# Four sigmoid gates of a hybrid layer: 512x1024x1024 products feature-major in eight blocks, or token-major with three of them by Strassen's seven products

## The chip, the core and the metric

The kernel runs on one core of a Trainium2 chip. The time is that of one execution on the device, in microseconds, and the number to compare is the median over several runs. On the core, TensorE (PE in the profile, with PEld for its weight loads) does the matrix products, VectorE (DVE) and ScalarE (ACT) do elementwise work, and transfers from DRAM are issued mostly on SyncE's queue (SP).

## The reference, cut to what matters

The kernel computes two blocks on 512 tokens of width 1024. The change touches the end of the second one:

```python
proj = h @ w_in                                   # h: 512 x 1024, normalised tokens
(..., gates) = jnp.split(proj, points, axis=-1)   # gates: 512 x 4096
ys = jnp.stack([y_a, y_b, y_c, y_d], axis=0)      # four branches, each 512 x 512
branch_d = jnp.einsum('nbsw,nwd->bsnd', ys, w_branch)
g = jax.nn.sigmoid(gates.reshape(bsz, s, N_BRANCH, d))
merged = jnp.sum(g * branch_d, axis=2)            # 512 x 1024
return x + merged @ w_out                         # then a last rms_norm
```

For each of four branches there is thus a gate, sigmoid of a product 512x1024x1024, and a branch product 512x512x1024 by which it is multiplied. The sum over branches goes through `w_out`; the block's own input `x`, the residual, is added.

## The kernel before, in words

**Arithmetic.** Every fp32 product is made of three passes in a reduced fp32 type: each operand is a high part and a low part, and high·high, high·low and low·high are summed in one PSUM bank (`mm3`; its matmuls all have line L264). The tokens are kept transposed, features on the partitions, as `HH` and `HL` (8 blocks of 128x512). A unit of work is a *piece* of weights, 128x1024 numbers: 8 blocks of 128x128 as stationary operand, with the tokens moving (feature-major result), or 2 blocks of 128x512 as moving operand, with the tokens stationary (token-major result). Either way a piece costs 24 matmuls of 512 columns when all 512 tokens take part.

**Weights.** SyncE's queue loads them, 1 MB at a time (two pieces), into three buffers `raw` (L207). For each piece ACT writes the high part, `whi` (L240), and DVE subtracts to get the low part, `wlo` (L241). `whi` and `wlo` are rings of WB = 3 pieces; the program order asks for the split of a piece LA = 2 pieces ahead of its matmuls (`wget`, `pump`), and a raw buffer is loaded anew when its last piece has been split (`used`).

**Order.** One list of items is run in order by `run`; at each item the side generators (`gmlp`, `topk`, `fox`, `dsa`, which make the branches' inputs) are advanced by a step. After the projections named in `MID` come the branches in the order `BRANCHES = (0, 2, 3, 1)`. For each, `gates(n)` gives four times: two gate pieces (`gt_item`, 24 matmuls each, one bank, evacuated by ACT's sigmoid) and one branch piece (`wb_item`, 24 matmuls, two banks, evacuated by DVE: multiply, L1612, and add to the running sum `mg`, L1617). So there are 32 gate pieces and 16 branch pieces. All results are feature-major: after the last branch each row block of `mg` is split in high and low part (`split_slot`: ACT, then DVE on L290) and is then the stationary operand of the last product, `wout_final("w2")`, 192 matmuls. Then `after2` adds the residual `XT`, which has lain in SBUF slots since the block's start, normalises and stores.

**Other names.** `presplit` splits the four inputs `yb` of a branch (L290). SBUF working tiles are slots of 128x512 fp32, `slot_...`; `CST` holds an identity for transposes on PE, which stand on L1108 and L1315 in this kernel.

Of the kernel before, what the change touches and what calls it, by code (L numbers as in the profile page):

```python
# [18 lines left out]
NT = S // 128  # L19
# [26 lines left out]

MID = ("ki qi0 qi1 au0 az0 au1 az1 au2 az2 au3 az3 dv dq0 dk0 dq1 dk1 bc bq0 dz0 dq2 dk2 bq1 cc0 cx0 cb0 cz0 "
# [3 lines left out]
def plan():  # L51


    def gates(n):
        r = []
        for p in range(4):
            r += [f"gt{n}_{2 * p}", f"gt{n}_{2 * p + 1}", f"wb{n}_{p}"]
        return r
# [14 lines left out]
    for n in BRANCHES:  # L73
        g += gates(n)
    g += [f"w2{h}_{j}" for j in range(4) for h in range(2)]
    g = [(n, 1024) for n in g]
    tail = [g[i:i + 2] for i in range(0, len(g), 2)]
# [6 lines left out]
def kernel(  # L84
# [98 lines left out]
    flat = []  # L183
    for r, items in enumerate(raws):
        o = 0
        for name, w in items:
            flat.append((name, r, o, w))
            o += w
    split_ids = {}
# [9 lines left out]
    ws = {"dma": 0, "split": 0, "next": 0}  # L199

    def dma_raw():
        r = ws["dma"]
        if r >= len(raws):
            return
        o = 0
        for w in [k for _, k in raws[r]] if r < 4 else [sum(k for _, k in raws[r])]:
            nc.sync.dma_start(raw_t[r % RAWB][:, o:o + w], wts[r, :, o:o + w])  # L207
            o += w
        ws["dma"] += 1

    def used(r):
        left[r] -= 1
        if left[r] == 0:
            dma_raw()

    def pump(upto):
        while ws["split"] <= min(upto, len(flat) - 1):
            i = ws["split"]
            name, r, o, w = flat[i]
            if i in in_slots:  # L220
                src = raw_t[r % RAWB]
                hs, ls = [get(), get()], [get(), get()]
                for kk in range(2):
                    c = slice(o + kk * 512, o + (kk + 1) * 512)
                    with tc.high_priority():
                        A.activation(hs[kk].r, src[:, c], AF.Copy)
                        V.tensor_sub(ls[kk].r, src[:, c], hs[kk].r)
# [4 lines left out]
            if i not in split_ids:  # L232
# [3 lines left out]
                continue  # L236
            s = split_ids[i] % WB
            src = raw_t[r % RAWB][:, o:o + w]
            with tc.high_priority():
                A.activation(whi[s][:, 0:w], src, AF.Copy)  # L240
                V.tensor_sub(wlo[s][:, 0:w], src, whi[s][:, 0:w])  # L241
# [13 lines left out]
    def adaget(name):  # L255
# [4 lines left out]
        return raw_t[r % RAWB], r  # L260


    def mm(o, l, r, start, stop):
        T.matmul(o, l, r, start=start, stop=stop)  # L264
# [765 lines left out]
    def wout_final(prefix, src, after):  # L1030


        presplit(src, range(8))
        bk = [[bget() for _ in range(2)] for _ in range(NT)]
# [774 lines left out]
```

## Time and profile before

| | |
|---|---|
| runs | 1137.42, 1135.6, 1137.52 us; median 1137.42 |
| the profiled execution: own time, span | 1135.7 us, 1133.9 us |
| PE busy | 1110.3 us, 98% of the span, 5253 matmuls |
| PE weight loads busy | 920.1 us, 81% |
| DVE busy | 726.1 us, 64% |
| ACT busy | 598.5 us, 53% |
| DMA | 118.5 MB, 105 GB/s over the span |

The profile shows one execution. Busy times are sums over instructions, where overlapping ones count once. An instruction's duration runs from its start to the end of its own results; instructions of one engine overlap, so the distance from one start to the next can be shorter than the duration. An engine is idle until the latest of what its next instruction needs has come. The stretch from about 809 to 1083 us of the span holds the gate products, and the last product follows until 1126 us.

### The profile page before, as it was taken

To read this page: it belongs to the slowest core of one execution; us is meant where nothing else is said; L and a number is where in the kernel's file an instruction comes from. 1 tells how busy PE (TensorE), PEld (TensorE's weight loads), DVE (VectorE), ACT (ScalarE), POOL (GpSimd) and SP (SyncE) were. 2 spreads that over 40 slices of the span, in tenths; PEclk is the share of its full clock that TensorE was granted. 3 is DMA by queue.
4 is the path that set the end of the run, shared out by engine and by line. 5 is a ranking of instruction groups with operands and counts; after the bars stand their busy time and mean duration, and the time that the engine had idled before them with its cause. 6 is when DMAs were issued, how large, how long until landed. Compare 5 with 4: busy or idle time off the path is not lost.

```text
span 1133.9 us, 13788 instructions
## 1 busy us (share of the span) xinstructions
PE 1110.3 (98%) x5253; PEld 920.1 (81%) x5253; DVE 726.1 (64%) x1476; ACT 598.5 (53%) x944; POOL 65.1 (6%) x73
## 2 busy tenths in 40 slices
PE   6999999999999999999999999999999999999997
PEld 4788888888878878788887888888888888888886
DVE  7977788763778556789798736555545434443435
ACT  6595497944677365553256434655766333223323
POOL 1330210101320000000000000000000000000000
PEclk9999999999999999999999999999999999999999
DMA  9734223223122452132232222222222322323202
GB/s 327 275 139 156 75 94 130 92 95 110 40 75 78 143 188 74 39 107 107 84 112 94 84 84 82 105 75 75 75 75 75 112 92 94 112 93 112 94 37 75
DMA packets 25422, 118.54 MB, mean 105 GB/s; under 512 B 2950, under 2 KB 3206, under 8 KB 13964
## 3 DMA queue, kind: packets, MB, share of 16 engines
q1 hardware_dynamic: 24780, 116.61, 29.3%
q10 hardware_dynamic: 576, 1.05, 0.2%
q8 instruction: 41, 0.67, 0.2%
q14 instruction: 25, 0.20, 0.1%
HBM read 115.54 MB, written 2.11 MB: 104 GB/s over the span
## 4 chain that ended last, share of the span: by engine, by line
PE 81%; DVE 9%; ACT 4%; issue 3%; POOL 2%; DMA 1%; SPq 0%; POOLq 0%; DVEq 0%; ACTq 0%
PE bank L264 79%; DVE slot L422 2%; ACT slot L105 1%; DVE slot L1267 1%; ACT whi L240 1%; ACT L105 1%; DVE wlo L241 1%; POOL slot L848 1%; DVE best L1266 1%; PE bank L1315 1%; DVE slot L290 1%; POOL slot L847 1%; DMA raw<-in_wts_dram 1%; DMA slot<-in_x_dram 0%; DVE slot L1079 0%
## 5 line engine op out<-in xcount | busy, mean ns | idle before, releaser
L264 PE MATMUL bank<-HH,whi 128*128 128x512 f32 x960 | 371.6, 394 | 1.4 <-ACT HH L105 1.2
L264 PE MATMUL bank<-HH,wlo 128*128 128x512 f32 x960 | 367.6, 390 | 0.0
L264 PE MATMUL bank<-HL,whi 128*128 128x512 f32 x960 | 366.2, 390 | 0.0
L240 ACT ACTIVATE whi<-raw 128x1024 fp32r<-128x1024 f32 (+1 forms) x170 | 178.7, 1052 | 310.6 <-PE bank L264 273.4
L241 DVE TENSOR_TENSOR wlo<-raw,whi 128x1024 fp32r<-128x1024 f32 (+1 forms) x170 | 206.4, 1215 | 194.6 <-ACT whi L240 185.7
L264 PEld LDWEIGHTS bank<-HH,whi 128*128 128x128 f32 x960 | 179.7, 188 | 40.3 <-ACT HH L105 4.4
L264 PEld LDWEIGHTS bank<-HH,wlo 128*128 128x128 f32 x960 | 180.2, 188 | 38.2
L264 PEld LDWEIGHTS bank<-HL,whi 128*128 128x128 f32 x960 | 180.3, 188 | 36.2
L105 ACT ACTIVATE slot<-slot 128x512 fp32r<-128x512 f32 (+4 forms) x179 | 100.5, 589 | 108.8 <-DVE slot L1660 26.0
L105 ACT ACTIVATE slot<-bank 128x512 f32<-128x512 f32 (+7 forms) x275 | 127.6, 491 | 43.5 <-PE bank L264 18.8
L264 PE MATMUL bank<-slot,slot 128*128 128x128 f32 (+5 forms) x755 | 133.5, 320 | 4.5 <-ACT slot L105 4.5
L264 PEld LDWEIGHTS bank<-slot,slot 128*128 128x128 f32 (+2 forms) x755 | 110.2, 186 | 20.1 <-issue 4.2
L105 ACT ACT_TABLE_LOAD x93 | 119.3, 1283 | 3.0 <-PEq L1798 0.7
L264 PE MATMUL bank<-slot,whi 128*128 128x512 f32 x272 | 85.4, 390 | 0.0
L264 PE MATMUL bank<-whi,slot 128*128 128x512 f32 x256 | 81.6, 394 | 0.2 <-ACT slot L105 0.2
L264 PEld LDWEIGHTS bank<-slot,whi 128*128 128x128 f32 x272 | 50.9, 188 | 10.8
L264 PEld LDWEIGHTS bank<-whi,slot 128*128 128x128 f32 x256 | 48.0, 188 | 10.9 <-ACT slot L105 1.1
L264 PE MATMUL bank<-slot,wlo 128*128 128x512 f32 x144 | 56.2, 390 | 0.0
L290 DVE TENSOR_TENSOR slot<-slot,slot 128x512 fp32r<-128x512 f32 x74 | 50.1, 685 | 9.4 <-ACT slot L105 9.2
L264 PE MATMUL bank<-wlo,slot 128*128 128x512 f32 x128 | 49.9, 390 | 0.0
L264 PE MATMUL bank<-whi,HL 128*128 128x512 f32 x120 | 47.1, 392 | 1.3 <-DVE HL L290 1.3
L264 PE MATMUL bank<-whi,HH 128*128 128x512 f32 x120 | 47.3, 394 | 0.6 <-ACT slot L105 0.5
(210 smaller groups left out, 1023.9 us busy)
## 6 DMA issues: line engine op xcount, KB each, us to landing
raw<-in_wts_dram SPq DMA_DIRECT2D x89, 1024.0 KB, 4.8
slot<-in_adw_dram SPq DMA_DIRECT2D x32, 256.0 KB, 6.3
slot<-in_x_dram SPq DMA_DIRECT2D x16, 256.0 KB, 4.5
raw<-in_wts_dram SPq DMA_DIRECT2D x8, 448.0 KB, 6.1
slot<-in_rows_dram SPq DMA_DIRECT2D x10, 256.0 KB, 3.8
slot<-CUM SPq DMA_DIRECT2D x4, 256.0 KB, 3.2
out_dram<-slot SPq DMA_DIRECT2D x4, 256.0 KB, 2.5
out_dram<-slot ACTq DMA_DIRECT2D x4, 256.0 KB, 2.3
```

The source lines that it names most:

```text
L105: return A.activation(o, i, func, **kw)
L240: A.activation(whi[s][:, 0:w], src, AF.Copy)
L241: V.tensor_sub(wlo[s][:, 0:w], src, whi[s][:, 0:w])
L264: T.matmul(o, l, r, start=start, stop=stop)
L290: V.tensor_sub(dst_l, src, dst_h)
L422: V.tensor_tensor_reduce(junk[i % 2].f, ada[k][i].f, cb[i % 2].f, 1.0, 0.0, ALU.mult, ALU.add, mds[k][:, i:i + 1])
L847: G.tensor_copy(d.f[:, 0:sh], src.f[:, 0:sh])
L848: G.tensor_add(d.f[:, sh:512], src.f[:, sh:512], src.f[:, 0:512 - sh])
L1266: V.max(best, sc.f[:, 0:n])
L1267: V.match_replace(sc.f[:, 0:n], best, sc.f[:, 0:n], MARK)
L1315: T.transpose(tb[:, cs], P[u1].f[:, cs], IDENT)
```

## The change

**Token-major gates.** Gate and branch product of all four branches are made with the tokens stationary and 512 output columns (a half) at a time. The first branch, 0, is a plain product (`plain_gate`, `wb_items`): 24 matmuls per piece as before, four banks per half.

**Seven products.** The gates of branches 2, 3 and 1 are cut in quarters, 256 tokens and 512 inputs by 512 inputs and 512 outputs, and made by Strassen's seven products in Winograd's form (`strassen_gate`, products in the order 1, 5, 6, 3, 7, 2, 4). A product has two pieces of 12 matmuls. The weights' combinations are formed in place in the raw buffers by DVE (`prep`) before they are split; the tokens' combinations S1 to S4 are formed once, by a new side generator in the first branch (`sums_work`), S4 in place of a quarter of `HH`, `HL`. Results are summed in PSUM where possible, copied by ACT or added by DVE where a part is used twice.

**Buffers.** As four raw quarters are in use at once, three more raw buffers, of four slots each, are added (`add_buf`); operations on them are 512 columns wide, two to a piece. To free slots, the residual is stored to DRAM (`XD`) after `av` and loaded again before `after2`.

**The sum transposed.** As `mg` is now token-major, `merged_T` transposes it on PE, 32 blocks of 128x128, in three places: 8 after each of the two pieces of product 4 of the last branch and 16 in the middle of the first half of the last product, which takes its pieces in another order.

The diff, cut to its core (`n` counts branches, `V` is DVE, `A` and `act` are ACT, `T` is PE):

```diff
+PRODUCTS = ((1, "11"), (5, "11"), (6, "11"), (3, "22"), (7, "12"), (2, "21"), (4, "11"))
...
+    n = BRANCHES[0]
+    for hf in (1, 0):
+        g += [f"gt{n}_{hf}_{j}" for j in range(4)] + half(n, hf)
+    pairs = [g[i:i + 2] for i in range(0, len(g), 2)]
+    for n in BRANCHES[1:]:
+        pairs += [[f"B{n}_11"], [f"B{n}_12"], [f"B{n}_22"], half(n, 1), [f"B{n}_21"], half(n, 0)]
+    pairs += [["w20_0", "w20_1"], ["w21_0", "w21_1"], ["w20_2", "w21_2"], ["w20_3", "w21_3"]]
+    tail = [[(n, 2048 if n[0] == "B" else 1024) for n in p] for p in pairs]
...
+            if name[0] == "B":
+                quarter[name[1:]] = r
+                n, q = name[1:].split("_")
+                for p, src in PRODUCTS:
+                    if (q == "22" and p not in (2, 4)) or (q == "21" and p in (2, 4)):
...
+        left[r] = {"11": 8, "12": 2, "22": 4, "21": 4}[name[-2:]]
...
+    def add_buf():
+        pool.append(Buf())
+        dma_raw()
...
+    def prep(i):
+        if i >= len(flat) or flat[i][0][0] != "P":
+            return
+        p, n, j = flat[i][0][1], flat[i][0][3], int(flat[i][0][5])
+        args = {"5": ("11", "12"), "6": ("11", "22"), "7": ("12", "22"), "4": ("11", "21")}.get(p)
+        if args is None:
+            return
+        rd, ra = (quarter[f"{n}_{q}"] for q in args)
+        d, a_ = raw_b[rd], raw_b[ra]
+        w = width(1024, d, a_)
+        for o in range(j * 1024, (j + 1) * 1024, w):
+            with tc.high_priority():
+                V.tensor_sub(d.at(o, w), a_.at(o, w), d.at(o, w))
+        if p in "74":
+            used(ra)
...
+            while ws["prep"] <= i + 1:
+                prep(ws["prep"])
+                ws["prep"] += 1
...
+                n = width(w, b)
+                for c in range(0, w, n):
+                    A.activation(whi[s][:, c:c + n], b.at(o + c, n), AF.Copy)
+                    V.tensor_sub(wlo[s][:, c:c + n], b.at(o + c, n), whi[s][:, c:c + n])
...
+        for n, (j, h) in enumerate(first):
+                if between and n == 2:
+                    between()
...
+    XD = dram.tile([512, 1024], F32, name="XD")
+    def x_block(t, h):
+        return XD[t * 128:(t + 1) * 128, h * 512:(h + 1) * 512]
+    for t in range(NT):
+        for h in range(2):
+            nc.sync.dma_start(x_block(t, h), XT[t, h].f)
+            put(XT.pop((t, h)))
...
+    def sums_work():
...
+        for q in range(2):
+            yield from room(6)
+            s1.append(get())
+            d = pair(s1, q)
+            V.tensor_add(d, qv(HH, 1, 0, q), qv(HH, 1, 1, q))
+            V.tensor_add(d, d, qv(HL, 1, 0, q))
+            V.tensor_add(d, d, qv(HL, 1, 1, q))
+            yield
+        for q in range(2):
+            yield from room(6)
+            s2.append(get())
+            d = pair(s2, q)
+            V.tensor_sub(d, pair(s1, q), qv(HH, 0, 0, q))
+            V.tensor_sub(d, d, qv(HL, 0, 0, q))
+            yield
+        yield from room(6)
+        split_sum("S1", s1)
...
+        while "plain" not in D:
+            yield
+        for q in range(2):
+            act(qv(HH, 1, 0, q), pair(s4, q), AF.Copy)
+            V.tensor_sub(qv(HL, 1, 0, q), pair(s4, q), qv(HH, 1, 0, q))
+        put(*s4)
+        sums["S4"] = True
+        while raw_more[0]:
+            yield from room(10)
+            add_buf()
+            raw_more[0] -= 1
+            yield
...
+            def mmf(j=j):
+                if j == 0:
+                    hold["b"] = [bget() for _ in range(NT)]
+                h, l = wget(f"gt{n}_{hf}_{j}")
+                for kk in range(2):
+                    k = 2 * j + kk
+                    c = slice(kk * 512, (kk + 1) * 512)
+                    for t in range(NT):
+                        ts_ = slice(t * 128, (t + 1) * 128)
+                        mm(hold["b"][t][:], HH[:, k, ts_], h[:, c], k == 0, False)
+                        mm(hold["b"][t][:], HH[:, k, ts_], l[:, c], False, False)
+                        mm(hold["b"][t][:], HL[:, k, ts_], h[:, c], False, k == 7)
...
+    def merged_T(hf, ks):
+        bs = [bget() for _ in ks]
+        for b, k in zip(bs, ks):
+            for t in range(NT):
+                T.transpose(b[:, t * 128:(t + 1) * 128], mg[t, hf].f[:, k * 128:(k + 1) * 128], IDENT)
+        for b, k in zip(bs, ks):
+            h, l = get(), get()
+            split(h.r, l.r, b[:])
+            merged[4 * hf + k] = h, l
...
+        def out(i, hf, part, banks_, free):
+            for t in range(2):
+                if part:
+                    s = part[t]
+                    V.tensor_add(s.f, s.f, banks_[t][:])
+                    act(s.f, s.f, AF.Sigmoid)
                 else:
...
+                    s = get()
+                    act(s.f, banks_[t][:], AF.Sigmoid)
+                if free:
+                    bput(banks_[t])
+                sg[2 * i + t, hf] = s
...
+                    h, l = wget(f"P{p}n{n}_{j}")
+                    for kk in range(2):
+                        k = 2 * j + kk
+                        c = slice(kk * 512, (kk + 1) * 512)
+                        for t in range(2):
+                            ah, al = stat(p, k, slice(t * 128, (t + 1) * 128))
+                            go = {} if opens else {"skip_group_check": True}
+                            mm(to[t][:], ah, h[:, c], opens and k == 0, False, **go)
+                            mm(to[t][:], ah, l[:, c], False, False, **go)
+                            mm(to[t][:], al, h[:, c], False, k == 3, **go)
+                def ev():
+                    if p == 1:
+                        copies(p1, X)
+                        presplit_yb(n)
+                    elif p == 5:
+                        copies(p5, Z)
+                    elif p == 6:
+                        copies(u2, X)
+                    elif p == 3:
+                        out(0, 1, u2, Z, True)
+                    elif p == 7:
+                        out(1, 1, p5, X, False)
+                    elif p == 2:
+                        out(0, 0, p1, Y, True)
+                    else:
+                        out(1, 0, None, X, True)
...
+        for p in (1, 5, 6, 3, 7):
+            r += product(p)
+        r += wb_items(n, 1) + product(2)
+        a4 = product(4)
+        if last:
+            a4 = [a4[0], (None, lambda: merged_T(1, (0, 1)), None), a4[1], (None, lambda: merged_T(1, (2, 3)), None)]
+        return r + a4 + wb_items(n, 0)
...
+    run(items, limit=4)
+    sides.append(sums_work())
+    n = BRANCHES[0]
+    items = []
+    for hf in (1, 0):
+        items += plain_gate(n, hf) + wb_items(n, hf)
+    for n in BRANCHES[1:]:
+        items += strassen_gate(n)
...
+    for t in range(NT):
+        for h in range(2):
+            XT[t, h] = get()
+            nc.sync.dma_start(XT[t, h].f, x_block(t, h))
...
-    wout_final("w2", merged, after2)
+    wout_final("w2", merged, after2, (4, 5, 6, 7, 0, 1, 2, 3), ((0, 0), (1, 0), (0, 1), (1, 1)),
+               lambda: merged_T(0, (0, 1, 2, 3)))
```

Three pieces of the program follow, before and after, in the order in which each engine executes. First DVE, before, in the gates of a branch; the names are those of the text above (`bank_` is PSUM):

```order
L241 TENSOR_TENSOR wlo_120<-raw_115,whi_117 128x1024
L241 TENSOR_TENSOR wlo_121<-raw_113,whi_118 128x1024
L1612 TENSOR_TENSOR slot_7092<-slot_7092,bank_63 128x512
L1617 TENSOR_TENSOR slot_6724<-slot_6724,slot_7092 128x512
L290 TENSOR_TENSOR slot_7557<-slot_6208,slot_7556 128x512
L290 TENSOR_TENSOR slot_7561<-slot_6264,slot_7560 128x512
L1612 TENSOR_TENSOR slot_7121<-slot_7121,bank_61 128x512
L1617 TENSOR_TENSOR span_6757<-span_6757,slot_7121 128x512
L241 TENSOR_TENSOR wlo_119<-raw_113,whi_116 128x1024
L241 TENSOR_TENSOR wlo_120<-raw_114,whi_117 128x1024
```

And DVE after, in the last branch, from the split of the first piece of product 6 (`wlo_121<-slot_6876`) to that of the first piece of product 3 (`wlo_120<-raw_113`); L309 is the split, L276 `prep`, here for product 4, L1801 and L1806 are multiply and add for the branch before:

```order
L309 TENSOR_TENSOR wlo_121<-slot_6876,whi_118 128x512
L1801 TENSOR_TENSOR slot_7603<-slot_7603,bank_67 128x512
L276 TENSOR_TENSOR slot_6876<-raw_114,slot_6876 128x512
L309 TENSOR_TENSOR wlo_121<-slot_6877,whi_118 128x512
L309 TENSOR_TENSOR wlo_119<-slot_6878,whi_116 128x512
L276 TENSOR_TENSOR slot_6877<-raw_114,slot_6877 128x512
L276 TENSOR_TENSOR slot_6878<-raw_114,slot_6878 128x512
L309 TENSOR_TENSOR wlo_119<-slot_6879,whi_116 128x512
L1806 TENSOR_TENSOR slot_6772<-slot_6772,slot_7603 128x512
L276 TENSOR_TENSOR slot_6879<-raw_114,slot_6879 128x512
L1801 TENSOR_TENSOR slot_7605<-slot_7605,bank_66 128x512
L309 TENSOR_TENSOR wlo_120<-raw_113,whi_117 128x1024
```

The splits of pieces were one operation of 1024 columns each, alone or around six operations of 512; now those of a quarter that lies in slots are two operations of 512 columns, and `prep`'s subtractions stand between them as well. From the split of product 5's first half piece to that of product 3's first piece there are 23 operations of 512 columns and the one of 1024.

PE before, from the last branch product to the last product:

```order
L264 MATMUL bank_61<-slot_7560,whi_116 128x512
L264 MATMUL bank_61<-slot_7561,whi_116 128x512
L264 MATMUL bank_61<-slot_7560,wlo_119 128x512
L264 MATMUL bank_68<-whi_117,slot_7621 128x512
L264 MATMUL bank_68<-wlo_120,slot_7621 128x512
L264 MATMUL bank_68<-whi_117,slot_7622 128x512
L264 MATMUL bank_64<-whi_117,slot_7621 128x512
L264 MATMUL bank_64<-wlo_120,slot_7621 128x512
L264 MATMUL bank_64<-whi_117,slot_7622 128x512
```

PE after, within product 4 of the last branch (L332 are the products' matmuls, L1817 the transposes of `mg`):

```order
L332 MATMUL bank_65<-whi_116,HH 128x512
L332 MATMUL bank_65<-wlo_119,HH 128x512
L332 MATMUL bank_65<-whi_116,HL 128x512
L1817 MATMUL bank_68<-CST,slot_6475 128x128
L1817 MATMUL bank_68<-CST,slot_6477 128x128
L1817 MATMUL bank_68<-CST,span_6479 128x128
L1817 MATMUL bank_68<-CST,slot_6481 128x128
L1817 MATMUL bank_64<-CST,slot_6475 128x128
L1817 MATMUL bank_64<-CST,slot_6477 128x128
L1817 MATMUL bank_64<-CST,span_6479 128x128
L1817 MATMUL bank_64<-CST,slot_6481 128x128
L332 MATMUL bank_62<-whi_117,HH 128x512
```

The last product followed the last branch product directly; now blocks of eight transposes, which read the sum's slots as DVE left them, stand between products of the last branch, and sixteen more inside the last product.

SP's queue before, at the end (L1024 loads the last normalisation's row, L207 weights, L1670 stores the output):

```order
L1024 DMA slot_7918<-in_rows_dram 128x512
L1024 DMA span_7917<-in_rows_dram 128x512
L207 DMA raw_113<-in_wts_dram 128x2048
L207 DMA raw_114<-in_wts_dram 128x2048
L207 DMA raw_115<-in_wts_dram 128x2048
L207 DMA raw_113<-in_wts_dram 128x2048
L207 DMA raw_114<-in_wts_dram 128x2048
L207 DMA raw_115<-in_wts_dram 128x2048
L207 DMA raw_113<-in_wts_dram 128x1024
```

SP's queue after, before the last weights (`XD` is the residual kept in DRAM):

```order
L1092 DMA slot_8107<-in_rows_dram 128x512
L1092 DMA slot_8106<-in_rows_dram 128x512
L1955 DMA slot_8110<-XD 128x512
L1955 DMA slot_8112<-XD 128x512
L1955 DMA span_8116<-XD 128x512
L245 DMA raw_113<-in_wts_dram 128x2048
L245 DMA slot_6853<-in_wts_dram 128x512
```

The loads of the residual stand between loads of weights, the first three of them ahead of `raw_113`, which holds the first pieces of the last product; each such load waits for its slot to be free.

## Rows read from the trace of the kernel before

**Rows 1.** The page: busy time of engines, and clock by slices.

```profile
PE 1110.3 (98%) x5253; PEld 920.1 (81%) x5253; DVE 726.1 (64%) x1476; ACT 598.5 (53%) x944; POOL 65.1 (6%) x73
...
PEclk9999999999999999999999999999999999999999
```

**Rows 2.** The page: the whole chain by line.

```profile
PE bank L264 79%; DVE slot L422 2%; ACT slot L105 1%; DVE slot L1267 1%; ACT whi L240 1%; ACT L105 1%; DVE wlo L241 1%; POOL slot L848 1%; DVE best L1266 1%; PE bank L1315 1%; DVE slot L290 1%; POOL slot L847 1%; DMA raw<-in_wts_dram 1%; DMA slot<-in_x_dram 0%; DVE slot L1079 0%
```

**Rows 3.** Chain from 880 us on: start, us, what.

```profile
879.90 246.67 PE bank L264 x1087
...
1126.60 0.70 DVE slot L1660
```

**Rows 4.** Stretches: length, then PE, PEld, DVE, ACT, POOL busy, clock, DMA, GB/s.

```profile
440.00:480.00 40.00, 38.49 (x182) 31.07 (x181) 33.57 (x95) 23.43 (x55) 0.00 (x0) 1.00 0.08 27
810.00:876.00 66.00, 66.00 (x320) 55.40 (x319) 31.31 (x65) 42.22 (x64) 0.00 (x0) 1.00 0.23 80
892.00:954.00 62.00, 62.00 (x275) 51.34 (x274) 27.04 (x32) 19.14 (x24) 0.00 (x0) 1.00 0.26 95
```

**Rows 5.** PE's timeline, tokens moving: start, us; 38 rows between.

```profile
903.14 0.39 PE L264 MATMUL bank<-HH,whi 128*128 128x512 f32 x1
...
911.98 0.39 PE L264 MATMUL bank<-HH,whi 128*128 128x512 f32 x1
```

**Rows 6.** PE's timeline, tokens stationary; 8 rows between.

```profile
556.14 0.39 PE L264 MATMUL bank<-wlo,HH 128*128 128x512 f32 x1
...
558.18 0.39 PE L264 MATMUL bank<-wlo,HH 128*128 128x512 f32 x1
```

**Rows 7.** PE's timeline at transposes, and all of that line (busy, mean ns).

```profile
467.72 1.47 PE L1108 MATMUL bank<-CST,slot 128*128 128x128 f32 x12
469.22 0.50 PE L264 MATMUL bank<-whi,HH 128*128 128x512 f32 x1
469.56 0.39 PE L264 MATMUL bank<-wlo,HH 128*128 128x512 f32 x1
...
L1108 PE MATMUL bank<-CST,slot 128*128 128x128 f32 x32 | 4.4, 274 | 0.0
```

**Rows 8.** DVE by line, 892 to 954 us: busy, mean ns, idle before.

```profile
L241 DVE TENSOR_TENSOR wlo<-raw,whi 128x1024 fp32r<-128x1024 f32 x12 | 14.7, 1223 | 30.7 <-ACT whi L240 30.7
L1612 DVE TENSOR_TENSOR slot<-slot,bank 128x512 f32<-128x512 f32 x8 | 5.5, 688 | 6.5 <-PE bank L264 6.5
L1617 DVE TENSOR_TENSOR slot<-slot,slot 128x512 f32<-128x512 f32 x7 | 4.8, 692 | 0.2
```

**Rows 9.** DVE's timeline where it works without a pause.

```profile
345.32 1.28 DVE L530 TENSOR_TENSOR slot<-slot 128x512 f32<-128x512 f32 x2
346.52 1.28 DVE L290 TENSOR_TENSOR slot<-slot,slot 128x512 fp32r<-128x512 f32 x2
...
349.24 1.23 DVE L241 TENSOR_TENSOR wlo<-raw,whi 128x1024 fp32r<-128x1024 f32 x1
350.38 0.69 DVE L647 TENSOR_TENSOR slot<-bank,CST 128x512 f32<-128x512 f32 x1
```

**Rows 10.** ACT by line, 892 to 954 us: busy, mean ns, idle before.

```profile
L240 ACT ACTIVATE whi<-raw 128x1024 fp32r<-128x1024 f32 x12 | 12.7, 1061 | 38.4 <-PE bank L264 34.5 <-issue 3.9
L105 ACT ACTIVATE slot<-bank 128x512 f32<-128x512 f32 x8 | 4.6, 579 | 0.0
```

**Rows 11.** DMA issues: KB each, median us to landing.

```profile
raw<-in_wts_dram SPq DMA_DIRECT2D x89, 1024.0 KB, 4.8
slot<-in_rows_dram SPq DMA_DIRECT2D x10, 256.0 KB, 3.8
```

More of the change, by code (lines that the diff above doesn't have):

```diff
@@ L51, in plan, with half @@
 def plan():
[L54 to L58, printed above, removed]
+    def half(n, hf):
+        return [f"wb{n}_{hf}_{j}" for j in range(2)]
     raws = []
@@ L1028, with wout_final @@
     xs = load_x()
-    def wout_final(prefix, src, after):
-        presplit(src, range(8))
-        bk = [[bget() for _ in range(2)] for _ in range(NT)]
-        for j in range(2):
-            for h in range(2):
+    def wout_final(prefix, src, after, korder=range(8), first=((0, 0), (0, 1), (1, 0), (1, 1)), between=None):
+        bk = [[None, None] for _ in range(NT)]
+        for n, (j, h) in enumerate(first):
[3 more added lines that the diff above has]
+                    for t in range(NT):
+                        bk[t][h] = bget()
                 wh, wl = wget(f"{prefix}{h}_{j}")
@@ new lines, in wb_items, with mmf, ev @@
+    def wb_items(n, hf):
+        hold = {}
+        items = []
+        for j in range(2):
+            def mmf(j=j):
+                while any((n, k) not in yb for k in range(4)):
+                    assert sides
+                    step_sides(4)
+                presplit_yb(n)
+                if j == 0:
+                    hold["b"] = [bget() for _ in range(NT)]
+                h, l = wget(f"wb{n}_{hf}_{j}")
+                for kk in range(2):
+                    k = 2 * j + kk
+                    c = slice(kk * 512, (kk + 1) * 512)
+                    yh, yl = yb[n, k]
+                    for t in range(NT):
+                        ts_ = slice(t * 128, (t + 1) * 128)
+                        b = hold["b"][t][:]
+                        mm(b, yh.r[:, ts_], h[:, c], k == 0, False)
+                        mm(b, yh.r[:, ts_], l[:, c], False, False)
+                        mm(b, yl.r[:, ts_], h[:, c], False, k == 3)
+                if j == 1 and hf == 0:
+                    for k in range(4):
+                        put(*yb[n, k])
+            def ev():
+                for t in range(NT):
+                    s = sg.pop((t, hf))
+                    V.tensor_mul(s.f, s.f, hold["b"][t][:])
+                    bput(hold["b"][t])
+                    if n == BRANCHES[0]:
+                        mg[t, hf] = s
+                    else:
+                        V.tensor_add(mg[t, hf].f, mg[t, hf].f, s.f)
+                        put(s)
+            items.append((None, mmf, ev if j == 1 else None))
+        return items
@@ new lines, in merged_T, with strassen_gate, need @@
+    def merged_T(hf, ks):
+        bs = [bget() for _ in ks]
+        for b, k in zip(bs, ks):
+            for t in range(NT):
+                T.transpose(b[:, t * 128:(t + 1) * 128], mg[t, hf].f[:, k * 128:(k + 1) * 128], IDENT)
[3 more added lines that the diff above has]
+            merged[4 * hf + k] = h, l
+            bput(b)
+        if ks[-1] == 3:
+            for t in range(NT):
+                put(mg.pop((t, hf)))
+    def strassen_gate(n):
+        X, Y, Z = [], [], []
+        p1, p5, u2 = [], [], []
+        last = n == BRANCHES[-1]
+        def need(name):
+            while name not in sums:
@@ L1655 @@
     ROW = load_row(6)
+    for t in range(NT):
+        for h in range(2):
+            XT[t, h] = get()
+            nc.sync.dma_start(XT[t, h].f, x_block(t, h))
     def after2(t, bk):
```

201 lines of the change are left out of this document (131 added, 70 removed).

## The prediction

> **What bounds the kernel now.** I read the page first. PE is busy for 98% of the span and its clock stands at the top step in every slice, DVE for 64%, ACT for 53% [rows 1]; the chain that ended last runs for 79% over the products' matmuls [rows 2]. Busy shares are means, so next I read the stretch of the change. From 880 us on the chain is one piece: 1087 matmuls in 246.67 us, with nothing between them, then a short tail on DVE and ACT [rows 3]. The table of stretches says the same from the other side: PE is busy for 66.00 of 66.00 us while the side work of the first branch still runs, and for 62.00 of 62.00 us after it; DVE has 31.31 and 27.04 us to do there, ACT 42.22 and 19.14 [rows 4]. So here a matmul left out is worth its whole distance to the next, 246.67 / 1087 = 0.2269 us, and an instruction of DVE or ACT costs nothing until it makes PE wait. The mean duration of a matmul (0.39 us) isn't its price, since neighbours overlap.
>
> **The sum, part by part.**
>
> *Matmuls removed.* A gate has 8 pieces of 24 matmuls, 192; by seven products it has 7 x 2 x 12 = 168. Three branches: 72 fewer. 72 x 0.2269 = -16.3 us. Branch 0 and all branch products keep their number.
>
> *Token-major instead of feature-major.* The weights change sides. With tokens moving, 39 matmuls took 911.98 - 903.14 = 8.84 us, 0.2267 each [rows 5]; with tokens stationary, in an earlier product of this kernel, 9 took 558.18 - 556.14 = 2.04 us, 0.2267 [rows 6]. Cost: none.
>
> *Transposes added.* There are 32. Twelve of the same shape and operands took 469.22 - 467.72 = 1.50 us, 0.125 each, and the first matmul behind them was followed after 0.34 us instead of 0.23 [rows 7]. So 32 x 0.125 = 4.0, and 3 groups x 0.11 = 0.3: +4.3 us. The row's mean duration, 0.274, is the other bound: 32 x 0.274 = 8.8 us. I take the distance, as this is a row of transposes on PE between matmuls, as here. The Trainium skill ("TensorE: Matmul & The Clock Gate", Part 4, PE-mode transpose) gives about 275 ns for such a transpose within a kernel, and says that it doesn't count as PE's work for the clock in the way that matmuls do. The duration agrees, the distance in the timeline doesn't; by the page's figure the transposes would be an estimated 8.8 us and the sum 4.5 us smaller. On the clock, the 40 us that hold all 32 of the old transposes show a granted clock of 1.00 [rows 4, 7].
>
> *DVE's new work.* A branch by seven products has 14 + 4 = 18 pieces to split instead of 12, 8 subtractions of a piece's size in `prep`, and 6 additions L1857 of a bank. By durations [rows 8] that is 27.0 + 6 x 1.22 + 8 x 1.22 + 6 x 0.69 = 48.2 us, in a stretch of 264 matmuls, or 59.9 us: 80%. ACT gets 6 copies of pieces at 1.06 and 6 copies of banks at 0.58 [rows 10], 19.1 + 9.8 = 29 us, half the stretch. In the first branch the sums S1 to S4 are some 28 operations at 0.69, 19 us, beside 31 of 66. So the means leave room, and the question is the order. DVE works without a pause at 0.60 us from start to start for 512 columns ((346.52 - 345.32) / 2) and 1.14 for 1024 (350.38 - 349.24) [rows 9].
>
> The tightest place that I find is in the last branch, where three quarters lie in slots. The split of product 5's first piece can start when the ring gets free, at the end of the branch product before. From there to the split of product 3's first piece stand 23 operations of 512 columns and one of 1024: 0.7 for ACT's copy + 23 x 0.60 + 1.14 = 15.6 us. PE meanwhile has 6 pieces of 12 matmuls, 6 x 2.72 = 16.3 us. It holds by 0.7 us; if the operations took their durations (23 x 0.69 + 1.22 + 0.7 = 17.8) PE would wait 1.5 us. In the branches before, fewer quarters lie in slots and the room is 2 us or more. I put 0.5 us here.
>
> *The first transposes* need the last addition for that half of the sum. After the branch product PE has products 2 and half of 4, 3 x 2.72 = 8.2 us; DVE has 12 operations of 512, 12 x 0.60 + 0.1 for the last one's end = 7.3 us, and starts up to 1 us late, since ACT and PE must be done. 0.3 us at most. The second group's operands are the same slots, and the 16 inside the last product need additions that are hidden behind 2 x 24 matmuls of it (10.9 us); what is late next there is the copy and the subtraction behind the transposes, about 0.6 + 0.7 us, with a bank's worth of transposes to hide them. Together +0.8 us for all waits.
>
> *Buffers and the residual.* The stores to DRAM wait for the residual's blocks in a stretch where DMA is busy for 0.08 of the time [rows 4]. The loads back stand ahead of the last product's weights on SP's queue, and wait for slots that the last reads of S1 to S3 set free, in products 5, 6 and 7 of the last branch. From product 7's end to the last product PE has 48 + 24 + 24 + 48 = 144 matmuls, 32.7 us; the split is asked for two pieces (10.9 us) ahead, which leaves 21.8 us. Even one after the other, three loads of 256 KB at 3.8 us and one of 1 MB at 4.8 us take 16.2 us [rows 11]. Cost: none; without that cover, PE would wait for up to 5 us. ACT's and DVE's splits of the sum (eight of each) were there before.
>
> *Sum.* -16.3 + 4.3 + 0.8 = -11.2 us. The profiled execution took 1135.7 us, so 1124.5. That run lay 1.7 us below the median of 1137.42, which two of three runs are near: 1126.2 on the median. I forecast **1126.0 us**.
>
> **Rivals.**
>
> *A. DVE late at several places.* For it: the room of 0.7 us above goes by the shortest distance that the trace shows, and DVE's rows wait for ACT's copies (L241's idle time ended there, 30.7 us [rows 8]). Against it: most of that wait is for PE to free the ring. At durations, the tightest place costs 1.5 us; up to that in each of three branches is 1 to 5 us: 1127 to 1132.
>
> *B. Transposes at their duration.* 8.8 instead of 4.0 us: 1126.0 + 4.8 = 1130.8. Against it stands the timeline; for it, that these read operands just written. The page on PE-mode transposes of the Trainium skill, named above, speaks for it too.
>
> *C. Copy and subtraction in series, which ends slower.* With the ring of three pieces, the split of a piece starts when PE leaves a buffer. In the stretch of products 1, 5, 6, 3 and 7 PE takes 10 x 2.72 = 27.2 us. DVE has 10 splits and 8 subtractions of `prep`, 18 x 1.14 = 20.5, and 12 operations of 512, 12 x 0.60 = 7.2: 27.7 us, so it can't catch up within that stretch, and lives on the lead that it has. If ACT's copy of 1.06 us came in series with each of the 10 splits, 10.6 us would be added, 11.1 over PE per branch, 33 in all: 1126 + 33 = 1159. It decides against the change from (11.2 + 2.3) / 3 = 4.5 us lost per branch, which is when four of ten copies are not ahead. For it: 27.7 against 27.2. Against it: ACT is half idle, and copies of the next pieces have 5.4 us of matmuls to run ahead in.
>
> *D. Less than the sum.* A tail as before, no wait, and a run like the fastest (1135.6 - 16.3 + 4.0): 1123.3. If a part of the change were a mere reordering it would be this: there, only the 72 and the 32 count.
>
> **How the numbers follow.** Forecast, 1124 to 1128: 0.66. A: 0.14. B: 0.06. C: 0.08, of which 0.02 end within 0.2% of the old time. D: 0.06. A measurement of this kernel can tell about 0.2%, 2.3 us, from no change. Faster by more: 0.66 + 0.14 + 0.06 + 0.06 = 0.92; within: 0.02; slower: 0.06. The range reaches down to D with a run's scatter (0.8 us) below, 1122.5, and up to where A ends, 1132.0; outside remain C and the thin ends of the others, about 0.12.
>
> **What would show it.** The chain in the gates and the last product should still be PE alone, and the matmuls there 72 fewer at 0.227. The 32 transposes, L1817, should stand 0.125 apart. PE's waits there should name, at most, `wlo` by DVE in the last branch around product 3 and the sum's slots before the first transposes, under 1 us together. DVE should be busy for some 48 of 60 us per branch. The prediction is wrong if PE waits for L309 at each product, for S sums in the second branch, for weights behind `XD`, or if the matmuls behind transposes keep a longer distance.

## The result, and the profile after

The changed kernel took 1122.78 us (median of 4 runs, 1121.48 to 1124.12), the kernel before 1136.51 beside it: ratio 0.988, 95% interval 0.9862 to 0.9898, that is 13.7 us less (11.6 to 15.7). Forecast were 1126.0 us and, from the same terms, 11.2 us less; the measured time lies inside the stated range, 0.3 us above its lower end.

The page of the kernel after, where it answers to [rows 1]:

```profile
span 1121.9 us, 14034 instructions
...
PE 1099.9 (98%) x5213; PEld 912.5 (81%) x5213; DVE 801.7 (71%) x1604; ACT 627.6 (56%) x1005; POOL 64.9 (6%) x73
```

PE has 10.4 us less to do, DVE 75.6 more, ACT 29 more, and the span is 12 us shorter: work was moved to engines that had time. The chain by time, from the first branch's last attention step on, answers to [rows 3] (start, length, what):

```profile
863.61 189.99 PE bank L332 x842
1053.59 0.87 PE bank L1817 x8
1054.47 2.74 PE bank L332 x12
1057.20 0.87 PE bank L1817 x8
1058.08 21.81 PE bank L332 x96
1079.89 1.75 PE bank L1817 x16
1081.64 32.97 PE bank L332 x144
```

PE alone is on the chain up to 1114.61 us, as before. In the timelines the first gate matmul stands at 810.87 us before and 811.51 after; by the chains the last matmul ends at 1126.57 and 1114.61. The stretch of the change takes 315.7 and 303.1 us, 12.6 less. The sum of the prediction gave 11.2, and its parts can now be read one by one. 72 matmuls at 0.2269 are 16.3. The transposes stand in the chain for 0.87 + 0.87 + 1.75 = 3.5 us, not 4.3. And the whole list of PE's waits from 620 us on is one row (waited for: us, times, longest), which the timeline puts ahead of the gates:

```profile
PE bank L332 <- ACT slot L110: 0.4, 1, 0.4
...
622.50 0.49 PE L332 MATMUL bank<-slot,slot 128*128 128x128 f32 x2 [0.40 <-ACT slot L110]
```

From 811 us on the list is empty: in the stretch of the change PE waits for nothing, where 0.8 us was put down. -16.3 + 3.5 = -12.8, within 0.2 of the 12.6. The rest of the 13.7 lies outside the stretch, within the scatter of runs (2.6 us in four).

The table of stretches (columns as in [rows 4]), roughly for the first branch and the three by seven products:

```profile
811.50:877.00 65.50, 65.50 (x318) 55.13 (x317) 39.09 (x79) 34.00 (x60) 0.00 (x0) 1.00 0.32 110
877.00:937.00 60.00, 60.00 (x267) 49.59 (x266) 45.72 (x56) 30.78 (x43) 0.00 (x0) 1.00 0.34 117
937.00:997.00 60.00, 60.00 (x266) 49.63 (x265) 49.84 (x68) 32.00 (x47) 0.00 (x0) 1.00 0.33 117
997.00:1057.00 60.00, 60.00 (x270) 49.68 (x269) 48.42 (x73) 30.70 (x49) 0.00 (x0) 1.00 0.35 121
```

DVE is busy for 46 to 50 of 60 us (48.2 was worked out), ACT for 31 to 32 (29). PE is busy throughout all four. (PE's own first products of the three branches stand at 887.27, 947.19 and 1007.11, some 10 us later than these stretches begin; cut there, DVE has 45 to 50 us in each.) So DVE at 80% doesn't show in the time. How near it is to showing is a question for the experiments.

### The profile page after: what moved, and what is told of

It reads as the page before. It is cut to its first block, busy times and chain, and to the rows that moved or that the text cites. A ratio compares the mean times of both kernels' runs of the same rounds, so it can differ in the third digit from the quotient of the medians.

```text
span 1121.9 us, 14034 instructions
## 1 busy us (share of the span) xinstructions
PE 1099.9 (98%) x5213; PEld 912.5 (81%) x5213; DVE 801.7 (71%) x1604; ACT 627.6 (56%) x1005; POOL 64.9 (6%) x73
## 4 chain that ended last, share of the span: by engine, by line
PE 81%; DVE 8%; DMA 3%; ACT 3%; issue 3%; POOL 2%; SPq 0%; POOLq 0%; DVEq 0%; ACTq 0%
PE bank L332 80%; DMA slot<-in_adw_dram 2%; DVE slot L1349 1%; ACT slot L110 1%; DVE best L1348 1%; ACT L110 1%; POOL slot L916 1%; ACT whi L308 1%; DVE slot L358 1%; DVE wlo L309 1%; PE bank L1397 1%; POOL slot L915 1%; DMA raw<-in_wts_dram 1%; DVE slot L490 1%; DMA slot<-in_x_dram 1%
## 5 line engine op out<-in xcount | busy, mean ns | idle before, releaser
L309 DVE TENSOR_TENSOR wlo<-raw,whi 128x1024 fp32r<-128x1024 f32 (+1 forms) x164 | 199.1, 1214 | 114.2 <-ACT whi L308 106.5
L332 PE MATMUL bank<-HH,whi 128*128 128x512 f32 x704 | 272.8, 397 | 1.2 <-ACT HH L110 1.0
L332 PE MATMUL bank<-HH,wlo 128*128 128x512 f32 x704 | 268.7, 392 | 0.0
L332 PE MATMUL bank<-HL,whi 128*128 128x512 f32 x704 | 267.7, 391 | 0.0
L332 PE MATMUL bank<-whi,slot 128*128 128x512 f32 x644 | 203.8, 391 | 0.0
L332 PEld LDWEIGHTS bank<-HH,whi 128*128 128x128 f32 x704 | 132.3, 189 | 30.6 <-ACT HH L110 4.2
L332 PEld LDWEIGHTS bank<-HH,wlo 128*128 128x128 f32 x704 | 132.7, 188 | 28.4
L332 PEld LDWEIGHTS bank<-HL,whi 128*128 128x128 f32 x704 | 132.9, 189 | 26.6
L332 PEld LDWEIGHTS bank<-whi,slot 128*128 128x128 f32 x644 | 120.9, 188 | 25.4 <-DVE slot L358 0.2
L332 PE MATMUL bank<-slot,slot 128*128 128x128 f32 (+5 forms) x748 | 131.7, 319 | 3.9 <-ACT slot L110 3.9
L332 PE MATMUL bank<-wlo,slot 128*128 128x512 f32 x328 | 127.8, 390 | 0.0
L332 PEld LDWEIGHTS bank<-slot,slot 128*128 128x128 f32 (+2 forms) x748 | 108.9, 186 | 19.1 <-issue 4.1
L332 PE MATMUL bank<-whi,HL 128*128 128x512 f32 x280 | 109.4, 391 | 1.4 <-DVE HL L358 1.3
L332 PE MATMUL bank<-whi,HH 128*128 128x512 f32 x280 | 109.9, 393 | 0.6 <-ACT slot L110 0.4
L332 PE MATMUL bank<-wlo,HH 128*128 128x512 f32 x280 | 109.1, 390 | 0.0
L332 PEld LDWEIGHTS bank<-wlo,slot 128*128 128x128 f32 x328 | 61.6, 188 | 12.6
L332 PEld LDWEIGHTS bank<-whi,HL 128*128 128x128 f32 x280 | 52.6, 188 | 13.0 <-DVE HL L358 2.0
L332 PEld LDWEIGHTS bank<-whi,HH 128*128 128x128 f32 x280 | 52.6, 188 | 12.1 <-ACT slot L110 0.9
```

What stands on the lines that cost most here:

```text
L309: V.tensor_sub(wlo[s][:, c:c + n], b.at(o + c, n), whi[s][:, c:c + n])
L332: T.matmul(o, l, r, start=start, stop=stop, **kw)
```

## The experiments

The theory: PE is the bound everywhere in this stretch, and the change is worth the matmuls left out less the transposes added, all else being hidden. Against it stand the rivals of the prediction, and one more: that the new order of operands, the residual's round trip or the extra buffers brought or cost something by themselves.

**The seven products undone.** All gates plain, the rest of the change kept:

```diff
+STR = ()
+PLAIN = tuple(n for n in BRANCHES if n not in STR)
...
-    for hf in (1, 0):
-        items += plain_gate(n, hf) + wb_items(n, hf)
-    for n in BRANCHES[1:]:
+    for n in PLAIN:
...
+        for hf in (1, 0):
+            gi = plain_gate(n, hf)
...
+            items += gi + wb_items(n, hf)
+    for n in STR:
         items += strassen_gate(n)
```

(merged_T's first two groups go between the last branch's pieces, and `sums_work` isn't started.)

> All four gates plain, token-major (24 matmuls a piece), no sums S1 to S4, no combinations of weights, no extra raw buffers; the sum is still transposed and the residual still goes through DRAM. Theory (only PE's own work counts: 72 matmuls at 0.227 us, 32 transposes at 0.11 us, all else hidden): the change's 1122.8 + 16.3 = 1139.1 us, that is 3.5 us or less above before's 1136.5; range 1138 to 1141. Rival (the new order of operands, or the freed slots, bring a part of the 13.7 us by themselves): 1136 or less. Rival (waits around the token-major form cost something that the seven products hide): over 1142.

Measured: 1139.29 us (before 1136.93 beside it, ratio 1.0021, 1.0011 to 1.003). 2.4 us slower than before, 16.5 slower than the change. The traces show it more closely, from the end of the attention in the first branch to the last matmul; the kernel before first, then this run (first and last piece of the stretch):

```profile
863.07 263.50 PE bank L264 x1166
...
862.72 192.62 PE bank L334 x854
...
1096.99 33.10 PE bank L334 x144
```

That is 263.50 us before and 267.37 here, 3.9 more, against 3.5 for the transposes; in the change it is 251.00 (863.61 to 1114.61). So everything but the seven products costs about what the transposes cost, and brings nothing; the whole gain comes from the 72 matmuls. (The medians differ by 1.5 us less than the stretches; this lies ahead of the gates or in the scatter of runs.)

**Seven products in one branch.** The last branch by `strassen_gate`, three plain.

> Seven products in the last branch alone, the other three plain. Theory (PE's own work): 24 matmuls fewer than all plain, 1139.1 - 5.4 = 1133.7 us, range 1132.5 to 1135. Rival (DVE is late in the last branch, where three quarters lie in slots, and gives back 1.5 to 4 us there): 1135 to 1138, and then the first two branches must have brought more than 5.4 each.

Measured: 1133.39 us (ratio 0.9971, 0.9959 to 0.9983). That is 5.9 below all plain, where 5.4 was expected, and the two other branches bring 1133.39 - 1122.78 = 10.6, 5.3 each. By the chains the stretch from the attention's end to the last matmul takes 261.96 us here (862.27 to 1124.23), 5.4 less than all plain, and 11.0 more than the change. The gain is linear in the branches; the last one, in which I had looked for lateness, gives nothing back.

**72 matmuls left out of the kernel before.** In three of eight gate pieces of three branches the third pass is left out.

```diff
+        short = name[0:2] == "gt" and name[2] != "0" and int(name[4]) in (2, 4, 6)
...
-            mm3(b[:], h[:, c], l[:, c], HH[:, k, :], HL[:, k, :], k == 0, k == 7)
+            mm(b[:], h[:, c], HH[:, k, :], k == 0, False)
+            mm(b[:], l[:, c], HH[:, k, :], False, short and k == 7)
+            if not short:
+                mm(b[:], h[:, c], HL[:, k, :], False, k == 7)
```

> The kernel before, with 72 matmuls left out and nothing else: in the last three branches three of eight gate pieces go without their third pass (weights high, tokens low), so these outputs lose the tokens' low parts. Theory (PE is the bound and a matmul left out is worth 0.227 us wherever it stands): 1136.5 - 16.3 = 1120.2 us. Rival (before, something else limits the gates, splits of weights or loads): less than 12 us gained, over 1124.5, and the change's 13.7 us came in part from elsewhere.

Measured: 1120.8 us, 16.1 less than before (ratio 0.986, 0.9845 to 0.9875). The change lies 2.0 us above that, no more than its transposes. The chain from the attention's end on takes 16.31 us less than the 263.50 of the kernel before:

```profile
864.56 247.19 PE bank L264 x1094
```

That is 0.2265 us for each of the 72. A matmul left out here is worth its distance to the next, whatever the reason for leaving it out.

**Transposes three times.**

```diff
-        for b, k in zip(bs, ks):
+        for b, k in [bk for bk in zip(bs, ks) for _ in range(3)]:
             for t in range(NT):
                 T.transpose(b[:, t * 128:(t + 1) * 128], mg[t, hf].f[:, k * 128:(k + 1) * 128], IDENT)
```

> Every transpose of the merged sum is done three times into the same place: 64 more, nothing else changed. Theory (a transpose costs its distance to the next in the timeline, 0.11 us): 1122.8 + 64 x 0.11 = 1129.8 us. Rival (it costs its whole duration, 0.272): 1122.8 + 17.4 = 1140.2. Rival (transposes fill waiting time and are hidden): 1122.8 to 1124.

Measured: 1129.29 us, 6.5 above the change: 6.5 / 64 = 0.10 us for each. The chain of this run shows the three groups at three times their length:

```profile
1054.25 2.62 PE bank L1817 x24
...
1059.61 2.62 PE bank L1817 x24
...
1084.04 5.24 PE bank L1817 x48
```

24 in 2.62 and 48 in 5.24 us is 0.109 each. That they cost their duration of 0.272 is refuted, and so is that they are hidden.

**More work for DVE.** First a half, then the whole of each subtraction of a product's piece is done twice into the same place:

```diff
                     V.tensor_sub(wlo[s][:, c:c + n], b.at(o + c, n), whi[s][:, c:c + n])
+                    m = 0 if c else 512
+                    if name[0] == "P" and m:
+                        V.tensor_sub(wlo[s][:, c:c + m], b.at(o + c, n)[:, 0:m], whi[s][:, c:c + m])
```

(In the second run `m = n`.)

> For each piece of the seven products DVE does the subtraction of the first 512 columns a second time into the same place: 14 operations of 0.60 us more per branch, 42 in all, PE's work unchanged. DVE then has 48 + 8.4 = 57 of 60 us per branch. Three theories. By means there is room: 1122.8. By the row of operations: between products 1 and 3 DVE takes about 2.9 us per piece against PE's 2.72, with 2.4 to 2.9 us of lead; 0.6 more on each of some five pieces uses up the lead and PE waits for 1 to 1.5 us per branch: 1124.5 to 1127.5. If DVE had no lead (copy and subtraction in series, the lead lost at the start of each branch), 10 x 0.6 - 0 = 6 us per branch, over 1135.

> The same with the whole subtraction done twice: 14 x 1.14 = 16 us more per branch, DVE 64 of 60 us. By means PE waits for at least 4 to 5 us per branch: 1135 to 1138. By the row of operations: 1.3 us too late per piece over seven pieces less the lead of 2.9, 4 to 6 us per branch: 1135 to 1141. If there is no lead, or lateness is not made good behind product 3: 10 us per branch and more, over 1150.

Measured: 1126.98 us (ratio 0.9913, 0.9898 to 0.9928) and 1143.59 us (1.0062, 1.0045 to 1.0079). With 25 us more for DVE, 4.2 are lost; with 48 more, 20.8. The first answers to the theory by the row of operations, 1124.5 to 1127.5, and not to the one by means: DVE had 53 us to do in the first stretch of 62, and 58 in the two later ones, and PE still waited. But that the number fits is in part luck, for I had put 1 to 1.5 us into each branch. PE's list of waits in the first of the two runs, from 862 us on, is this alone (behind it the table of stretches there):

```profile
PE bank L335 <- DVE wlo L312: 2.3, 1, 2.3
...
875.00:937.00 62.00, 59.70 (x263) 48.85 (x262) 52.95 (x69) 30.24 (x43) 0.00 (x0) 1.00 0.33 111
```

The timeline puts the end of the wait at 904.27 us, in the second piece of product 6 of the first branch by seven products; in the two later branches, where DVE has more to do, PE waits for nothing. From the attention's end to the last matmul this trace is 3.1 us longer than the change's; the wait is 2.3 of that. (In this run's timeline two matmuls of product 3 stand on PE ahead of this wait, which isn't so in the change: the program's order differs a little too, so the run isn't a pure dose for DVE.) The second run is worse than both of my better theories, 1135 to 1141. There PE's list, from 862 us on, is:

```profile
PE bank L335 <- DVE wlo L312: 8.0, 7, 3.6
PE bank L335 <- DVE slot L361: 2.8, 1, 2.8
PE bank L335 <- ACT slot L110: 1.1, 2, 0.6
PE bank L335 <- ACT whi L308: 0.7, 1, 0.7
```

PE waits seven times for the doubled subtraction, and the longest of these waits is followed by something else. The table of stretches of this second run, around it:

```profile
964.00:972.00 8.00, 6.78 (x28) 5.34 (x29) 7.82 (x10) 2.72 (x5) 0.00 (x0) 1.00 0.07 19
972.00:980.00 8.00, 4.41 (x11) 3.16 (x11) 8.00 (x14) 1.75 (x3) 0.00 (x0) 0.66 0.61 210
```

After 3.59 us without work the granted clock has a mean of 0.66 over 8 us, between the levels of 1.2 and 2.4 GHz. The waits named in the list come to 12.6 us of the 20.8. Behind the longest, eleven matmuls stand 0.43 us apart instead of 0.23 (976.63 to 981.32), some 2.2 us more by that difference; the rest isn't resolved.

**One more buffer instead of three; and the residual left where it was.** First `raw_more = [1]` alone; then this, and the residual's stores and loads taken out, so that it keeps its eight slots.

> One more raw buffer instead of three (four in all), the residual still through DRAM. Theory (loads of 4.8 us are hidden with four buffers too, and PE is alone on the chain): 1122.8, range 1121.5 to 1124.5; the operations 1024 wide instead of two of 512 relieve DVE a little. Rival (the additional buffers are what keeps the weights in time, PE waits for a quarter in each of three branches for 2 us or more): over 1128.

> One more raw buffer instead of three, and the residual stays in SBUF: no stores to DRAM and no loads back (16 transfers of 256 KB fewer). Theory (the round trip is hidden and costs nothing): the same as with one more buffer and the round trip, 1121.5 to 1124.5. Rival (the loads back stand ahead of the last product's weights or disturb, and cost 2 us or more): 2 us or more below that run. Rival (without the eight slots the sums S1 to S4 or the fourth buffer come too late): over 1128.

Measured: 1122.76 us (ratio 0.9876, 0.9861 to 0.9891) with four buffers, the same as with six, and 1124.94 us (0.9894, 0.988 to 0.9909) without the round trip, 2.2 slower. So four buffers keep PE fed as well as six, and the round trip through DRAM brings no loss: the run without it is the slower one. The chain of that last run leaves PE once in the gates, in the first branch by seven products:

```profile
901.75 1.07 ACT whi L308
902.84 1.23 DVE wlo L309
904.06 0.60 DVE slot L1710
904.66 0.61 DVE HL L1718
905.32 149.31 PE bank L332 x656
```

L1718 writes S4's low part, which product 3 reads. With eight slots fewer the sums are made later: DVE writes this part at 862.74 and 874.06 us in the change, and at 904.58 here, when PE is at product 3. From the attention's end to the first transposes this run takes 190.5 us against 190.0. I found 0.9 us of the 2.2 in the gates and the last product together (251.86 against 251.00); the rest lies ahead of the attention's end, which comes at 864.09 us here and at 862.89 with four buffers and the round trip, and its cause stays open.

**Seven products in all four branches.** An attempt at a faster kernel: the sums are begun before the gates, eight or (second run) sixteen items ahead of the projections' end. One more raw buffer is added instead of three, and each step of the sums waits for 12 or (second run) 16 free slots instead of 6.

```diff
+STR = (0, 2, 3, 1)
...
-            yield from room(6)
+            yield from room(12)
...
-    raw_more = [3]
+    raw_more = [1]
...
+    items.insert(len(items) - 8, (None, lambda: sides.append(sums_work()), None))
     run(items, limit=4)
-    sides.append(sums_work())
...
+    D["plain"] = True
...
+    for n in STR:
         items += strassen_gate(n)
```

> Seven products in all four branches: the sums S1 to S4 are begun eight items before the end of the projections, where DVE is busy half of the time, S4 is written when the projections are done, and one more raw buffer instead of three serves. Theory (PE's own work alone): 24 matmuls fewer, 1122.8 - 5.4 = 1117.4 us. By the row of DVE's operations the first branch would have the attention's operations beside 48 us of splits and combinations in 60, and lose 1 to 4 us of this: 1118 to 1121. Rival (DVE, with less than 3 us of lead, falls behind there for the whole branch): 1122.8 or more, no gain.

> The same with the sums begun sixteen items before the end of the projections and a larger reserve of free slots before each step of them. If what is lost in the run before is lost to sums that stand between the first branch's splits, this is 1 to 3 us faster than that run, 1117.4 to 1119; if it is lost to the attention's operations in the first branch, the two are within 1 us of each other. Rival (the sums then disturb the projections, where PE has waited for nothing): slower than the run before.

Measured: 1127.41 us (0.9916, 0.9901 to 0.9931) and 1129.17 us (0.993, 0.9914 to 0.9947). Both are slower than the change, by 4.6 and 6.4 us, with 24 matmuls fewer: my sums fell, and the first run's rival, no gain, came true. The second isn't faster than the first. That the sums disturb the projections there is excluded, for PE waits for nothing from 700 to 810 us; but the sums aren't cleared either, for where its chain leaves PE longest in the gates, from 843.86 to 850.53 us, parts of S3 (L1720 to L1722) stand beside `prep` (L278). The table of stretches of this second run, then its chain:

```profile
760.00:810.00 50.00, 50.00 (x247) 42.14 (x246) 32.65 (x72) 31.31 (x53) 0.00 (x0) 1.00 0.18 64
...
845.21 0.60 DVE slot L1722
...
847.01 2.27 DVE raw L278 x2
849.28 0.60 DVE slot L1721
```

PE's list of waits from 700 us on, for the first of them:

```profile
PE bank L1399 <- DVE slot L1368: 5.4, 1, 5.4
PE bank L334 <- ACT slot L112: 0.5, 1, 0.5
```

L1399 and L1368 belong to the attention, not to the gates. In the changed kernel the attention's last transposes on PE stand at 863.17 us (x4); here, in the chain, at 841.35:

```profile
841.35 1.13 PE bank L1399 x4
```

It advances by a step at each item of the list, a branch by seven products has more items than a plain one, and where a product lacks its sum, all side generators are stepped until it is there. So its steps crowd, and it finds DVE busy with splits and combinations: in the chain two `prep` operations (L278, 2.27 us) stand ahead of L1368. And again the clock follows, in the table of stretches of the same run:

```profile
836.00:844.00 8.00, 2.11 (x7) 1.42 (x8) 6.75 (x14) 3.59 (x10) 0.00 (x0) 0.63 0.15 62
844.00:850.00 6.00, 6.00 (x23) 5.19 (x23) 4.60 (x9) 2.58 (x6) 0.00 (x0) 0.64 0.00 0
```

That the crowding is the cause rests on these rows alone, and how much the sums add to it wasn't separated; a version that spreads the attention over a first branch by seven products was not run, so whether a fourth branch can be had at a gain stays open.

## Why the prediction was right, point by point

**The number.** The forecast lies 3.2 us above the measured time: 0.7 in the time of the kernel before (1126.0 + 11.2 = 1137.2 against 1136.51), 2.5 in the difference (11.2 against 13.7). Of these 2.5 the transposes make 0.8 and the waits 0.8, both put down too high; the rest lies outside the stretch. The measured time lies below the 1124 to 1128 us to which 0.66 was given; the range holds because it was drawn down to rival D. So the mechanism was right, and two small terms were too large.

**The bound.** PE alone on the chain, in the stretch of the change too: shown by the chain, and by the two runs in which matmuls were left out or put back (-16.1 and +16.5 us for 72; 16.3 was worked out from [rows 3]).

**The order of operands costs nothing** [rows 5, 6]: all plain, token-major, is 2.4 us above before, less than the transposes' 3.5, and 3.9 above it in the traces' stretch, which leaves 0.4 us at most for the order.

**Transposes.** Taken at 0.125 us and 0.3 us for the groups' ends, 4.3 in all; measured at 0.109 with the ends, 3.5. The row that this came from [rows 7] holds the same 0.109: its twelve take 1.47 us from the first's start to the last's end, and without the last's duration of 0.27 these are 11 distances. What was dearer there is the block's end: the second matmul behind it (469.56) starts 0.30 us later than twelve distances and one of a matmul's make. In the changed kernel's timeline eight stand between 1053.43 and 1054.22, and the second matmul behind them (1054.54) comes 0.01 us later than by this count:

```profile
1053.20 0.39 PE L332 MATMUL bank<-whi,HL 128*128 128x512 f32 x1
1053.43 0.38 PE L1817 MATMUL bank<-CST,slot 128*128 128x128 f32 x2
...
1054.22 0.48 PE L332 MATMUL bank<-whi,HH 128*128 128x512 f32 x1
1054.54 0.40 PE L332 MATMUL bank<-wlo,HH 128*128 128x512 f32 x1
```

The first starts at 1053.43 and the eighth at 1054.19, 7 distances of 0.109; the mean duration is again 272 ns. The Trainium skill's figure of about 275 ns in a kernel ("TensorE: Matmul & The Clock Gate", Part 4, PE-mode transpose; its measurement in isolation is of bf16) agrees with the duration here, and would have been 2.5 times too dear as a price. The 32 old transposes of [rows 7] are those of L1108 alone; the kernel before has 80 more on L1315, with the same median of 272 ns, and no term hung on it. On the clock, the stretch with the first sixteen, from the table of stretches, shows 1.00:

```profile
1050.00:1058.00 8.00, 8.00 (x45) 6.80 (x44) 6.99 (x13) 7.01 (x13) 0.00 (x0) 1.00 0.01 2
```

**Waits.** 0.8 us was put down, none was there. The place that I took for the tightest had more room than I gave it. In the timelines of the kernel after, ACT starts the split of product 5's first half piece in the last branch here:

```profile
1004.63 0.63 ACT L308 ACTIVATE whi<-slot 128x512 fp32r<-128x512 f32 x1 [2.09 <-PE bank L332]
```

DVE starts the subtraction for product 3's first piece here:

```profile
1019.33 1.22 DVE L309 TENSOR_TENSOR wlo<-raw,whi 128x1024 fp32r<-128x1024 f32 x1
```

And PE comes to that piece here:

```profile
1023.51 0.39 PE L332 MATMUL bank<-whi,HH 128*128 128x512 f32 x1
```

DVE is done at 1020.55, 3.0 us ahead, where I had 0.7. The duration of the row of operations was right (15.6 worked out, 15.9 measured). What failed is the start: I let it begin when PE had left the whole ring buffer, 6 x 2.72 = 16.3 us before use, but it began 18.9 us before use. The pieces in slots are split in halves, and a half is free as soon as PE has left that half: ACT takes these two halves at 1004.63 and 1007.36, twelve matmuls of PE apart. Nor is it the tightest place. In the first two branches by seven products the second piece of product 6 has less room: in the first of them DVE ends this split at 898.47 us and PE first uses its low part at 901.17, 2.7 us later (2.6 in the next branch, and 3.2 by the same count at the place above):

```profile
897.25 1.22 DVE L309 TENSOR_TENSOR wlo<-raw,whi 128x1024 fp32r<-128x1024 f32 x1
...
901.17 0.39 PE L332 MATMUL bank<-wlo,slot 128*128 128x512 f32 x1
```

This is the piece at which PE waited under the half dose.

**The rivals.** DVE late (A): not in this kernel, but the half dose shows how near it is: 0.6 us more per piece brings it, in the first branch by seven products. Transposes at their duration (B): refuted. Copy and subtraction in series (C) didn't make PE wait; the whole dose, with 7 us lost per branch, shows what it takes to turn the sign. A mere sum without waits (D), 1123.3: this is the one that came nearest, with a chance of 0.06. It came nearest on the time and on the waits, while its 0.125 for a transpose was too high as well. I gave too much weight to waits that I could name but not show; an account of PE's own rows would have been better by itself.

## What to carry to other kernels

Where one engine is alone on the chain, count its instructions and take each at its distance to the next, not at its duration: four such sums here, for matmuls and transposes put in and left out, came within 0.6 us. The same sum for the attempt with four branches missed by 10 us (1117.4 against 1127.41), as PE wasn't alone there. An engine at 80% busy beside it can hold, but its room is what lies between the split's end and its use at the tightest place, 2.6 us in the branches by seven products, and neither a share nor a mean shows it: doubling a known operation measures it. Before a reduction of work is extended to a place where side work runs, look at what else is paced by the number of items there.

## What the runs showed of the hardware that I had not expected

Transposes of 128x128 fp32 in a block on PE stand 0.109 us apart, with a duration of 0.272. A wait of 3.6 us of PE was followed by a stretch with a mean granted clock of 0.66, and in the attempt with four branches the 14 us around and behind a wait of 5.4 us have 0.63 and 0.64. Behind that wait the matmuls of 512 columns stand 0.43 us apart (846.32, 846.74, 847.17), which is the level of 1.2 GHz; at 2.4 they stand 0.23 apart. These two waits cost more than their length. Not every wait did: around the 2.3 us of the half dose (899 to 906 and 906 to 912 us) the granted clock is 1.00.
